# Convolutions ahead of the pooling branch, the samples' recurrence inside it, and one product of keys with q and k

## The chip, the core and the metric

The kernel runs on one core of a Trainium2 chip. Its time is the device time of one execution in microseconds; the figure that counts is the median of several runs. Five engines work side by side: TensorE (PE, with its weight loads as PEld), VectorE (DVE), ScalarE (ACT), GpSimd (POOL) and SyncE (SP), which here only issues DMAs. Each engine works through its own instructions in order and waits on semaphores for the others.

## What is computed

One inference step of a hybrid decoder layer, for a prompt of 1024 tokens and for 8 samples of 4 tokens each (1056 columns in all), everything in float32. Cut to what matters here:

```python
def mixer_layer(x, p_i, conv_hist, s0, pool_hist, pos0, ...):
    h = rmsnorm(x, norm_mix)
    q_r, k_r, v_r, z, a_r, b_r, u, gp, ga, gb = jnp.split(h @ w_in, IN_SPLITS, axis=-1)
    qkv, conv_new = causal_conv(concat([q_r, k_r, v_r]), conv_hist, conv_w)   # 4 taps, silu
    q, k = l2norm(q) * HEAD_K ** -0.5, l2norm(k)                              # 8 heads of 128
    g, beta = -exp(a_log) * softplus(a_r + dt_bias), sigmoid(b_r)
    o, s_new = gated_delta_chunked(q, k, v, g, beta, s0, chunk)               # needs k.k and q.k
    y_a = (rmsnorm(o, gdn_norm) * silu(z)) @ w_proj_a
    y_pool, pool_new = pool_mix(u, pool_hist, pos0, pool_w, pool_scale)       # windows 2, 4, 8, 16
    y_b = (y_pool * silu(gp)) @ w_proj_b
    m = sigmoid(ga) * y_a + sigmoid(gb) * y_b
    x = x + m @ w_out
    return x + sigmoid(rmsnorm(x, norm_ple) @ w_ple_gate) * (p_i @ w_ple_proj), ...
```

The prompt starts from empty state; each sample brings a convolution history, a pooling history and a 128x128 recurrent matrix for each head, and its new states are outputs too.

## The kernel before, in words

Activations lie with features on the 128 partitions and tokens along the row, in three chunks of 352 columns. A dense product takes one output tile of 128 features (`dense`, L378): each of the three chunks is 24 matmuls (`chunk`, L306), because each operand is split into a high and a low part in the format fp32r (`hh`, `hl` for activations, `wh`, `wl` for weights) and three of the four products are made for each of the eight 128-row blocks. So a dense tile is 72 matmuls of 352 columns. The weights of a tile come by a 512 KB DMA into one of two `wr` buffers (`fetch`), ScalarE copies them to `wh` and GpSimd subtracts to get `wl` (`split_w`), one tile ahead. Products inside the heads are plain float32 and appear in the trace as two passes of TensorE each; transposes are one pass.

The order of the instructions on every engine but SP is written out by hand through a planner (`Weave`, L74). It keeps a planned time for every engine from a table of costs (`COST`, and the ns handed to `mm`), runs the dense tiles as the main line, and between any two matmuls steps those side threads (Python generators) that are due by the planned time (`pump`). A `mark` is a planned finishing time, `until` and the lists that threads yield wait for marks. Rings hand out buffers (`take`, `give`). The planner's times only fix the order; on the chip each instruction waits for its real inputs.

The stages, in order:

1. Start (to about 59 us): `w_ple_proj` products, the first norm, splitting of h.
2. Convolutions and pooling (to about 546 us). For m = 0 to 7: the dense tile of u (`w_in` 32+m), whose evacuation by ScalarE fills the one buffer `up`; thread `windows` (DVE sums over 2, 4, 8 or 16 tokens, then `shi`, `slo`); at even m the group map of the previous group (`group_maps`, 36 matmuls); then the tiles k (8+m, through `conv_tile(m, 1)`), gate (40+m), q (m) and v (16+m). A conv tile is evacuated by ScalarE into `xr`; two DVE steps a chunk add the middle taps to `acc`, GpSimd adds `f`, ScalarE makes a tanh, DVE multiplies; the result goes to DRAM (`kq_d`, `v_d`). Buffers: two `xr`, three `f`, one `acc` for each chunk. Dense products have four PSUM banks here (`psd`).
3. Heads (to about 1143 us). The main line is 8 tiles of z, 15 of gates and 8 of `w_proj_b`, with two `psd` banks. Side threads take the heads in four pairs (`pair`, `decays`, `whole`, `queries`, `values`, `recurrence`): load k, transpose, products k.k, inverse of a triangular matrix (DVE), load q, products q.k, load v, a recurrence over 8 chunks of 128 tokens, output to `og_d`. All their big buffers are 19 slots of 4 KB a partition (`U_r`, `NSLOT`). Pair p+1 starts when pair p has all its slots (mark `have`). After them thread `samples` runs the recurrence of the 8 samples: it waits for the last pair's `have` and for z, takes seven slots and `en`, loads 4 MB of states in 256 KB pieces and writes them back, and ends in `osm` (mark `smp`).
4. At m = 2 to 7 of `w_proj_b` the program asks whether all heads and the samples are done; if so, or after the last tile, `heads_end` frees the heads' memory and the threads `reload` bring `og_d` back in 24 pieces (`rw`), split into `oh` and `ol`, the input of `w_proj_a`.
5. `w_proj_a`, `w_out`, the norm, `w_ple_gate`, final norm (to the end).

Of the kernel before, what the change touches and what calls it, by code (L numbers as in the profile page):

```python
# [18 lines left out]
P = 128  # L19
# [24 lines left out]
NSLOT = 19  # L44
# [190 lines left out]
def decoder_step(ctx, tc, A, O):  # L235
# [110 lines left out]
    order += [("pool_w", 3)] + [("w_in", 24 + m) for m in range(H)] + [("w_in", 49 + m) for m in range(2 * KT - 1)] + [("w_proj_b", m) for m in range(KT)]  # L346
# [340 lines left out]


    with pool("pw", 2) as pw, pool("cvt") as cv, pool("psab", 2, space=PSUM) as psab:
        wv.add(token_rates(ab, abf, psab))  # L690
        ring = lambda p, name, shape, n, dt=F32: Ring(wv, [p.tile(shape, dt, name=f"{name}{i}") for i in range(n)])
# [6 lines left out]
        yh_r, yl_r = (ring(cv, f"ys{x}", [P, CW], 3, F32R) for x in "hl")  # L698
# [57 lines left out]
        seg4 = lambda t: t.rearrange("p (s x) -> p s x", x=7)[:, :, 0:ST]  # L756

        def conv(n, c, o, h, j, xr, f):

            m = 8 * j + h  # L760
            c0, c1 = n * CW, (XW - 3 if n == 2 else (n + 1) * CW)
            if n < 2:
                S.copy(xr[:, 3 + c0:3 + c1], o)
            else:
                xs = xr[:, 3 + TP:XW]
                S.copy(xr[:, 3 + c0:3 + TP], o[:, 0:TP - c0])
                S.copy(xs.rearrange("p (s x) -> p s x", x=7)[:, :, 3:7],
                       o[:, TP - c0:CW].rearrange("p (s x) -> p s x", x=ST))
            yield "ps"
            act = yield from acc_r[n].take()  # L770
            yield
            acc = act[:, 0:c1 - c0]
            fc = f[:, c0:c1]
            S.activation(acc, xr[:, c0:c1], AF.Copy, scale=cw[:, m, 0:1])
# [7 lines left out]
            if n == 2:  # L782
                G.tensor_copy(cvp[:, m, :], xr[:, TP:TP + 3])
                SY.dma_start(O["conv_s"][:, m], xs)
# [281 lines left out]
    def recurrence(o):  # L1066
# [7 lines left out]
        for u in range(NU):  # L1074
# [27 lines left out]
            if u:  # L1102
                mm(po[:, P:2 * P], Fq[:, tok], st, 222)
# [657 lines left out]
```

## Time and profile before

| | us |
|---|---|
| median of 3 runs | 1467.9 |
| lowest and highest of them | 1463.51, 1471.36 |
| the profiled execution's own time | 1464.74 |
| its span, first to last instruction | 1463.0 |
| mean granted TensorE clock | 0.986 of 2.4 GHz |

The profile is one execution of the program. The page gives each engine's busy time; the views cut it by stretch of time, by line, by tile and by wait. In the name of a tile the buffer number is left out; helpers record all dense and head matmuls as L247, transposes as L251, all ScalarE, DVE and GpSimd work as L186 and DMA issues as L231, so groups are told apart by tile. Names of the heads' buffers appear as `U`. The end of a matmul is modelled: it includes the way through the array, so matmuls overlap in the listing, and the distance from one start to the next is what one costs. Most of the loss on TensorE is therefore read from counts of matmuls in a stretch, beside the idle time that the view shows.

### The profile page before, as it was taken

To read this page: it belongs to the slowest core of one execution; us is meant where nothing else is said; L and a number is where in the kernel's file an instruction comes from. 1 tells how busy PE (TensorE), PEld (TensorE's weight loads), DVE (VectorE), ACT (ScalarE), POOL (GpSimd) and SP (SyncE) were. 2 spreads that over 40 slices of the span, in tenths; PEclk is the share of its full clock that TensorE was granted. 3 is DMA by queue.
4 is the path that set the end of the run, shared out by engine and by line. 5 is a ranking of instruction groups with operands and counts; after the bars stand their busy time and mean duration, and the time that the engine had idled before them with its cause. 6 is when DMAs were issued, how large, how long until landed. Compare 5 with 4: busy or idle time off the path is not lost.

```text
span 1463.0 us, 24635 instructions
## 1 busy us (share of the span) xinstructions
PE 1410.1 (96%) x9266; PEld 1369.5 (94%) x9266; DVE 844.0 (58%) x1779; ACT 590.9 (40%) x1545; POOL 427.1 (29%) x353
## 2 busy tenths in 40 slices
PE   9899999999999998999999999999899699999996
PEld 8799999999999998999999999999799599999996
DVE  6675564565657653474663764665665554556655
ACT  6344444444444444536536436525101322324321
POOL 3524433334343441411313212301332011315100
PEclk9999999999999999999999999999999899999998
DMA  9223243142224228241441431495265644424132
GB/s 333 61 65 94 69 130 100 58 136 87 86 71 135 79 73 249 99 107 44 159 132 54 170 124 36 163 289 173 88 208 166 219 142 133 136 67 128 46 96 88
DMA packets 106235, 178.95 MB, mean 122 GB/s; under 512 B 19260, under 2 KB 78852, under 8 KB 106116
## 3 DMA queue, kind: packets, MB, share of 16 engines
q1 hardware_dynamic: 106116, 177.37, 37.9%
q8 instruction: 73, 1.20, 0.3%
q14 instruction: 46, 0.38, 0.1%
HBM read 119.92 MB, written 57.41 MB: 121 GB/s over the span
## 4 chain that ended last, share of the span: by engine, by line
PE 87%; DVE 7%; DMA 2%; ACT 2%; issue 1%; SPq 0%; POOL 0%; DVEq 0%; ACTq 0%; POOLq 0%
PE psd L247 73%; PE psr L247 6%; PE psg L247 5%; PE psg L251 2%; DVE U L186 1%; DMA rw<-og_d 1%; DVE win L186 1%; PE pse L247 1%; DVE hl L186 1%; DVE ol L186 0%; DMA xt<-in_xT_dram 0%; DVE x L186 0%; DVE sg L186 0%; DVE tm L186 0%; SPq L231 0%
## 5 line engine op out<-in xcount | busy, mean ns | idle before, releaser
L247 PE MATMUL psd<-hh,wh 128*128 128x352 f32 x1728 | 569.9, 330 | 2.6 <-DVE sg L186 2.0
L247 PE MATMUL psd<-hl,wh 128*128 128x352 f32 x1728 | 566.7, 328 | 0.0
L247 PE MATMUL psd<-hh,wl 128*128 128x352 f32 x1728 | 565.0, 327 | 0.0
L186 POOL TENSOR_TENSOR wl<-wr,wh 128x1024 fp32r<-128x1024 f32 (+1 forms) x87 | 207.3, 2383 | 551.8 <-ACT wh L186 508.5
L247 PEld LDWEIGHTS psd<-hh,wh 128*128 128x128 f32 x1728 | 326.8, 189 | 5.2 <-issue 2.1
L247 PEld LDWEIGHTS psd<-hl,wh 128*128 128x128 f32 x1728 | 327.3, 189 | 1.4 <-issue 0.2
L247 PEld LDWEIGHTS psd<-hh,wl 128*128 128x128 f32 x1728 | 326.7, 189 | 1.5 <-issue 0.5
L186 DVE SCALAR_TENSOR_TENSOR acc<-xr,cw,acc 128x352 f32<-128x352 f32 x144 | 123.6, 868 | 60.9 <-ACT acc L186 59.3
L186 POOL TENSOR_TENSOR acc<-acc,f 128x352 f32<-128x352 f32 (+1 forms) x72 | 78.6, 1092 | 118.9 <-DVE acc L186 84.3
L186 ACT CAST wh<-wr 128x1024 fp32r<-128x1024 f32 (+1 forms) x88 | 90.5, 1028 | 14.9 <-issue 7.4
L186 DVE SCALAR_TENSOR_TENSOR f<-f,acc 128x352 f32<-128x352 f32 (+1 forms) x72 | 60.9, 849 | 46.0 <-ACT f L186 46.0
L186 ACT ACTIVATE junk<-psg 128x128 f32<-128x128 f32 (+1 forms) x136 | 38.5, 283 | 85.8 <-PE psg L251 71.0
L247 PE MATMUL psd<-oh,wh 128*128 128x352 f32 x192 | 64.0, 333 | 7.6 <-ACT oh L186 7.6
L247 PE MATMUL psd<-ol,wh 128*128 128x352 f32 x192 | 64.5, 336 | 5.6 <-DVE ol L186 5.4
L186 ACT COPY xr<-psd 128x352 f32<-128x352 f32 (+1 forms) x96 | 34.0, 380 | 81.0 <-PE psd L247 80.9
L186 ACT ACTIVATE gt<-psd 128x352 f32<-128x352 f32 x69 | 32.5, 472 | 82.4 <-PE psd L247 69.8
L247 PE MATMUL psd<-oh,wl 128*128 128x352 f32 x192 | 63.6, 331 | 0.0
L186 ACT ACTIVATE f<-acc 128x352 f32<-128x352 f32 (+1 forms) x72 | 36.2, 503 | 47.1 <-POOL acc L186 32.4
L186 DVE SCALAR_TENSOR_TENSOR gt<-gt,psd 128x352 f32<-128x352 f32 x48 | 24.8, 516 | 49.1 <-ACT gt L186 33.6
L186 ACT COPY U<-psr 128x128 f32<-128x128 f32 (+1 forms) x68 | 18.1, 270 | 83.2 <-PE psr L247 35.0
L251 PE MATMUL psg<-cst,U 128*128 128x128 f32 (+3 forms) x272 | 40.7, 274 | 8.5 <-DVE U L186 5.2
L247 PE MATMUL psd<-gh,rh 128*128 128x352 f32 x144 | 46.8, 325 | 0.0
(256 smaller groups left out, 2564.0 us busy)
## 6 DMA issues: line engine op xcount, KB each, us to landing
wr<-in_w_in_dram SPq DMA_DIRECT2D x64, 512.0 KB, 3.9
kq_d<-f SPq DMA_DIRECT2D x16, 512.0 KB, 2.9
U<-kq_d SPq DMA_DIRECT2D x16, 512.0 KB, 5.5
xt<-in_xT_dram SPq DMA_DIRECT2D x6, 704.0 KB, 7.2
pp_d<-ppt SPq DMA_DIRECT2D x24, 176.0 KB, 5.8
yh_d<-ysh SPq DMA_DIRECT2D x24, 176.0 KB, 3.5
yl_d<-ysl SPq DMA_DIRECT2D x24, 176.0 KB, 2.6
tb_d<-gt SPq DMA_DIRECT2D x24, 176.0 KB, 1.8
```

The costliest lines, as they stand in the source:

```text
L186: return f(*a, **k)
L247: PE.matmul(o, l, r, start=start, stop=stop)
L251: PE.transpose(o, i, idn)
```

## The change

Three things are changed together.

- **Order.** All 24 conv tiles come first, head by head in the order q, k, v, with three `xr`, four `f` and two `acc` for each chunk; the planner drains its threads and the last convolution state is written. Then come the pooling tiles alone: u, at even m the group map, gate.
- **Samples.** `samples` keeps its instructions but runs as a side thread of the pooling stage, with buffers of its own in a pool `smp` and two PSUM rings of two banks (`sg`, `sr`), and waits neither for heads nor for z. Its last step no longer multiplies by silu(z): ScalarE writes `osm`, and after the last z tile GpSimd multiplies `osm` by `ssz`; the mark `smp` is set there.
- **Heads.** q and k of a head are loaded together into one buffer F of two rows (four such buffers of 8 KB; the 4 KB slots go from 19 to 13). The products k.k and q.k of a chunk become one matmul of 256 columns with k stationary, two of them to a PSUM bank; each bank is read by two DVE products of 256 columns. `queries` keeps only transposes and squares. v's slot and load come ahead of the inverse.

The diff, cut to its core (the body of `samples`, `group_maps` and `windows` is moved and is the same line for line where nothing is shown):

```diff
-NSLOT = 19
+NSLOT = 13
-    order = [("w_in", 48)]
+    order = [("w_in", 48)] + [("w_in", h + 8 * j) for h in range(H) for j in range(3)]
     for m in range(KT):
-        order += [("w_in", 32 + m)] + [("pool_w", m // 2 - 1)] * (m > 1 and m % 2 == 0)
-        order += [("w_in", 8 + m), ("w_in", 40 + m), ("w_in", m), ("w_in", 16 + m)]
+        order += [("w_in", 32 + m)] + [("pool_w", m // 2 - 1)] * (m > 1 and m % 2 == 0) + [("w_in", 40 + m)]
...
-        xr_r = ring(cv, "xr", [P, XW], 2)
-        f_r = ring(cv, "f", [P, XW], 3)
-        acc_r = [ring(cv, f"acc{n}_", [P, XW - 2 * CW], 1) for n in range(NCH)]
+        xr_r = pring(cv, "xr", [P, XW], 3)
+        f_r = pring(cv, "f", [P, XW], 4)
+        acc_r = [pring(cv, f"acc{n}_", [P, XW - 2 * CW], 2) for n in range(NCH)]
...
+        for h in range(H):
+            for j in range(3):
+                conv_tile(h, j)
+        wv.until()
+        SY.dma_start(O["conv_p"], cvp)
+    actx.close()
+    with pool("smp") as smp, pool("pw", 2) as pw, ExitStack() as pc:
+        g_r, r_r = banks(pc, "sg", 2), banks(pc, "sr", 2)
...
-        yield [("have", H // 2 - 1), ("z", H - 1)]
-        slots = []
-        for _ in range(7):
-            slots.append((yield from U_r.take()))
-        yield from en_r.take()
...
-        V.scalar_tensor_tensor(out=osm, in0=pf[:, 0:H * TS].rearrange("p (h t) -> p h t", t=TS), scalar=gn,
-                               in1=ssz.rearrange("p (h t) -> p h t", t=TS), op0=ALU.mult, op1=ALU.mult)
-        wv.mark("smp")
+            S.activation(osm, pf[:, 0:H * TS].rearrange("p (h t) -> p h t", t=TS), AF.Copy, scale=gn)
...
+        wv.add(samples())
         last, grp = None, None
         for m in range(KT):
...
-            conv_tile(m, 1)
-            conv_tile(m, 0)
-            conv_tile(m, 2)
...
     U_r = ring("U", [P, NU, P], NSLOT)
+    F_r = ring("F", [P, 2, TP], 4)
...
-            o.Fk = flat((yield from U_r.take()))
-            SY.dma_start(o.Fk, kq_d[o.h][1], ("k", o.h))
+            o.F = yield from F_r.take()
+            SY.dma_start(o.F[:, 1], kq_d[o.h][1], ("k", o.h))
+            SY.dma_start(o.F[:, 0], kq_d[o.h][0], ("q", o.h))
...
-            for g in range(2):
-                yield [("decay", o.h, g)]
+            for g in range(4):
+                yield [("decay", o.h, g // 2), ("q", o.h)]
                 pk = yield from g_r.take()
                 yield
-                for j in range(4):
-                    mm(pk[:, j * P:(j + 1) * P], o.Fk[:, tok], o.Fk[:, tok], 222)
-                V.tensor_tensor(out=o.nt[:, us], in0=units(pk), in1=en[:, i, us], op=ALU.mult)
+                for j in range(2):
+                    mm(pk[:, 2 * j * P:2 * (j + 1) * P], o.F[:, 1, tok], o.F[:, :, tok], 240)
+                V.tensor_tensor(out=o.nt[:, us], in0=pv[:, :, 1], in1=en[:, i, us], op=ALU.mult)
+                V.tensor_tensor(out=o.em[:, us], in0=pv[:, :, 0], in1=o.em[:, us], op=ALU.mult)
...
-                mm(pq[:, i * P:(i + 1) * P], o.Fk[:, tok], o.Fq[:, tok], 222)
-            V.tensor_tensor(out=em[:, us], in0=units(pq), in1=em[:, us], op=ALU.mult)
...
+                if h == H - 1:
+                    yield
+                    G.tensor_tensor(out=osm, in0=osm, in1=ssz.rearrange("p (h t) -> p h t", t=TS), op=ALU.mult)
+                    wv.mark("smp")
```

## Rows read from the trace of the kernel before

**Rows 1.** The page: busy us, share of the span and instructions of each engine.

```profile
PE 1410.1 (96%) x9266; PEld 1369.5 (94%) x9266; DVE 844.0 (58%) x1779; ACT 590.9 (40%) x1545; POOL 427.1 (29%) x353
```

**Rows 2.** Stretches: busy us (instructions) of PE, PEld, DVE, ACT, POOL; clock; DMA.

```profile
59.00:541.00 482.00, 480.68 (x3021) 479.18 (x3022) 283.77 (x402) 218.40 (x440) 183.62 (x173) 1.00 0.28 89
541.00:566.00 25.00, 19.80 (x111) 18.96 (x110) 11.88 (x21) 9.37 (x25) 7.14 (x5) 0.92 0.69 227
566.00:1025.00 459.00, 451.37 (x3324) 435.08 (x3323) 259.05 (x762) 220.65 (x807) 103.40 (x85) 1.00 0.42 133
1025.00:1143.50 118.50, 112.17 (x711) 103.28 (x709) 70.71 (x151) 15.01 (x33) 39.90 (x32) 0.99 0.47 153
1143.50:1171.50 28.00, 14.86 (x57) 12.79 (x56) 14.97 (x34) 12.50 (x33) 2.54 (x1) 0.72 0.77 252
```

**Rows 3.** Waits of PE, 1143.5 to 1171.5: total us, times, longest.

```profile
PE psd L247 <- ACT oh L186: 7.6, 1, 7.6
PE psd L247 <- DVE ol L186: 5.4, 3, 3.1
```

**Rows 4.** Groups of PE, 1025 to 1143.5.

```profile
L247 PE MATMUL psd<-hh,wl 128*128 128x352 f32 x161 | 53.6, 333 | 0.0
L247 PE MATMUL psr<-en,U 128*128 128x128 f32 x64 | 11.0, 298 | 1.5 <-DVE U L186 1.5
L247 PE MATMUL psg<-ue,kl 96*128 96x512 f32 x16 | 7.2, 452 | 0.6 <-DVE ue L186 0.6
```

**Rows 5.** Timeline of PE, heads stage: start us, us, what, count.

```profile
611.06 1.05 PE L247 MATMUL psg<-U,U 128*128 128x128 f32 x8
...
612.11 0.33 PE L247 MATMUL psd<-hl,wh 128*128 128x352 f32 x1
```

**Rows 6.** Tile psg on PE, 1000 to 1143: ns minimum/median/maximum, first and last start.

```profile
L247 PE MATMUL psg<-ue,kl x16: 393/474/501, 1065.8 to 1131.3; 96*128 96x512 f32 x16
L251 PE MATMUL psg<-cst,sq x12: 270/272/273, 1008.4 to 1017.1; 128*64 128x128 f32 x12
```

**Rows 7.** Timeline of SP's queue at 1040 us: the last output of a head.

```profile
1040.28 0.32 SPq L231 DMA_DIRECT2D og_d<-U  x1
```

**Rows 8.** Groups of PE, 1040.5 to 1143.5: count, busy us, mean ns, idle before.

```profile
L247 PE MATMUL psd<-hh,wl 128*128 128x352 f32 x144 | 48.0, 333 | 0.0
```

**Rows 9.** Groups of DVE, 60 to 541: the pooling windows.

```profile
L186 DVE TENSOR_TENSOR win<-up 128x1190 f32<-128x1190 f32 x8 | 11.2, 1398 | 44.5 <-ACT up L186 44.5
L186 DVE TENSOR_TENSOR slo<-y,shi 128x1056 fp32r<-128x1056 f32 x8 | 10.6, 1319 | 4.1 <-ACT shi L186 3.9
```

**Rows 10.** DMA issues, 1000 to 1143: count, KB each, median us to landing.

```profile
out_delta_s_dram<-U SPq DMA_DIRECT2D x8, 256.0 KB, 2.1
```

**Rows 11.** Stretches view: two conv tiles back to back.

```profile
104.00:127.00 23.00, 23.00 (x146) 23.00 (x146) 14.64 (x18) 13.22 (x27) 10.32 (x11) 1.00 0.25 74
```

**Rows 12.** Waits of PE, 541 to 566.

```profile
PE psg L251 <- DMA U<-kq_d: 3.3, 1, 3.3
PE psd L247 <- DVE sg L186: 1.9, 2, 1.0
```

**Rows 13.** Timeline of PE at the norm's broadcast product (352 columns, plain float32).

```profile
1292.31 0.76 PE L247 MATMUL pse<-dg,cst 88*128 88x352 f32 x2
...
1293.06 0.32 PE L247 MATMUL psd<-ml,wh 128*128 128x352 f32 x1
```

**Rows 14.** Groups of DVE, 566 to 1025: a product that reads a whole bank.

```profile
L186 DVE TENSOR_TENSOR U<-psg,en 128x512 f32<-128x512 f32 x16 | 11.0, 690 | 18.1 <-PE psg L247 16.7 <-DMA out_delta_p_dram<-st 1.1
```

**Rows 15.** Groups by line, 60 to 541: conv tiles' DVE and GpSimd work, weight split.

```profile
L186 DVE SCALAR_TENSOR_TENSOR acc<-xr,cw,acc 128x352 f32<-128x352 f32 x141 | 121.8, 874 | 60.9 <-ACT acc L186 59.3
L186 POOL TENSOR_TENSOR wl<-wr,wh 128x1024 fp32r<-128x1024 f32 (+1 forms) x43 | 101.3, 2357 | 175.5 <-ACT wh L186 151.7 <-ACT acc L186 9.5 <-issue 9.2
L186 POOL TENSOR_TENSOR acc<-acc,f 128x352 f32<-128x352 f32 (+1 forms) x70 | 76.7, 1096 | 114.3 <-DVE acc L186 82.2 <-ACT f L186 23.7 <-DVE y L186 3.1
L186 DVE SCALAR_TENSOR_TENSOR f<-f,acc 128x352 f32<-128x352 f32 (+1 forms) x69 | 59.4, 864 | 45.8 <-ACT f L186 45.8
```

More of the change, by code (lines that the diff above doesn't have):

```diff
@@ L754, in windows @@
             wv.mark("win", m)
[L756 to L770, printed above, removed]
[L771 to L778 removed]
+        R = 64
@@ new lines, in chain @@
+                pb = yield from g_r.take()
+                for a in range(2):
+                    mm(pb[0:96, a * P:(a + 1) * P], f3(x3[:, a]), r, 222)
+                if g:
+                    yield [("sn", g - 1)]
+                V.tensor_tensor(out=u3, in0=units(pb[0:96, 0:2 * P]),
+                                in1=d3[:, 0:8].rearrange("p (a g) -> p a g", a=2)[:, :, g].unsqueeze(2).broadcast_to([96, 2, P]),
+                                op=ALU.mult)
+                g_r.give(pb)
+                yield
@@ new lines, in chain @@
+                uu = r_
+                S.copy(ul, u3)
+                for a in range(2):
+                    V.tensor_copy(uu[32 * a:32 * a + 32], u3[32 * a:32 * a + 32, a])
+                yield
+                V.tensor_tensor(out=ul[32:64], in0=u3[32:64], in1=ul[32:64].bitcast(F32), op=ALU.subtract)
+                po = yield from g_r.take()
+                mm(po[0:R, 0:P], sk[:, g], uu, 222)
+                V.tensor_tensor(out=oo[:, g, :], in0=po[0:R, 0:P], in1=oo[:, g, :], op=ALU.add)
@@ new lines, in chain, with products @@
+                g_r.give(po)
+                wv.mark("ch", g)
+                yield [("kl",)]
+                yield from new_states(g)
+            def products(g):
+                pa = yield from r_r.take()
+                for i in range(16):
+                    if i % ZN == 0:
+                        yield
+                        c = slice(R * g + ST * i, R * g + ST * (i + ZN))
+                        V.tensor_copy(cols(0), s8(sq[:, 1, c]))
+                        V.tensor_tensor(out=cols(R), in0=s8(sq[:, 0, c]), in1=s8(gbs[:, g, ST * i:ST * (i + ZN)]), op=ALU.mult)
+                        yield
+                    if i % 4 == 0:
+                        yield [("sg", g, i // 4)]
+                    c = 60 + P * (i % ZN) - ST * i
+                    mm(pa[:, 0:P], zf[:, c:c + P], sgs[g % 2][i // 4][:, i % 4, :], 222, start=(i == 0), stop=(i == 15))
+                    if i % 2:
+                        yield AHEAD
+                wv.mark("pa", g)
+                return pa
@@ L785, in conv @@
+            wv.add(states(2))
+            wv.add(states(3))
+            for g in range(4):
+                pa = yield from products(g)
+                if g:
+                    yield [("ch", g - 1)]
+                wv.add(chain(g, pa))
+                yield
+            yield [("ch", 3), ("sn", 3)]
+            at[0] = 160
+            ss = t_([R, 4], "sss")[0:R]
+            for g in range(4):
+                S.activation(r_, oo[:, g, :], AF.Square, accum_out=ss[:, g:g + 1])
             yield
-            S.activation(fc, acc, AF.Tanh, scale=0.5)
+            ro = yield from out_scale(R, 4, ss, n2[:, 0, :], t_)
@@ L795, in conv @@
[L795 to L810 removed]
+            pf = yield from g_r.take()
```

558 lines of the change are left out of this document (254 added, 304 removed).

## The prediction

> **What bounds the kernel now.** I read the page first: TensorE is busy for 96% of the span, no other engine for more than 58% [rows 1]. So two questions decide: does the change take work from TensorE, and does it take away gaps? The stretches view shows where the gaps are. A dense pass (352 columns, fp32r) costs 480.68 us / 3021 = 0.159 us in the convolution and pooling stage, where TensorE hardly ever stands still; I use 0.160 [rows 2]. With that price a stretch's loss is its length less its passes. From 1143.5 to 1171.5 there are 57 passes, 9.1 us of work in 28.0 us: 18.9 us are lost, 13 as idle time and the rest because the clock was at 1.2 instead of 2.4 GHz for part of it, a mean of 0.72 [rows 2]. The waits name the cause: `oh` and `ol`, the reloaded outputs of the heads [rows 3]. From 1025 to 1143.5, the samples' stretch, I count three groups of about 161 dense passes (77.0 us), 128 passes of `psr` at 0.111, priced below (14.2), 16 of `ue` at an estimated 0.3 (4.8: between a dense pass scaled to 512 columns, 0.23, and the listed mean of 0.45) and 86 others of at most 0.111 (9.5): at most 105.5 us, so at least 13.0 us are lost, of which 118.5 - 112.2 = 6.3 show as idle [rows 2, 4]. From 541 to 566, where the heads begin, 111 passes are at most 17.8 us of 25: 7.2 lost [rows 2]. The 459 us of the heads show 7.6 us idle [rows 2]; the start and the end are not touched.
>
> **The reload, 17.9 us off.** Before, `heads_end` could not come before `smp`, and the samples' last product starts at 1131 [rows 6], when `w_proj_b` was nearly through; so all 24 pieces were reloaded with TensorE waiting. The heads themselves were done earlier: the last `og_d` leaves at 1040 [rows 7], and from there to 1143.5 three groups of 144 dense passes remain, exactly six tiles, 6 x 11.5 = 69 us [rows 8]. With `smp` set after the z tiles, the program can call `heads_end` near tile m = 2 or 3 of `w_proj_b`, and 28 us of reload fit beside 58 or more us of dense work. DVE, busy 71 of 118 us there with the samples, loses their part [rows 2]. I keep 1 us for the new PSUM banks. If heads ended 45 us later, that cover would be gone and all 18.9 us would be back. Bounds: 15 to 18.9. The same loads now queue on SP among the `tb` loads that evacuations need, so I charge 1 us (0 to 3).
>
> **The samples, 3.1 us off.** The same passes of TensorE, ScalarE, DVE and GpSimd work, 16 loads and 16 stores of 256 KB on SP move into the pooling stage. That stage has 16 dense tiles and 144 group-map passes, 16 x 11.5 + 23 = 207 us of TensorE without the samples; the chain's products ran from 1008 to 1131 us before, 123 us [rows 6], so it ends in time. What of the loss comes along? The 6.7 us that do not show as idle are short gaps between small products; they come along. Of the 6.3 us of idle I let half come along: these are steps whose DVE work was later than planned, and the pooling windows put 1.4 us instructions in their way [rows 9], but four PSUM banks, not two, serve the dense tiles. So 13.0 - 6.7 - 3.2 = 3.1 us. Bounds: from -8 (each of the 16 blocks of state products held up by half a window instruction, 0.7 us) to +13. SP is a queue in order: a state's reload waits for its store to land, 2.1 us [rows 10], four times in a row, and weights, `y_d` stores and pooling histories stand behind. Weights are fetched a tile ahead, 11.5 us; I cost this at nothing, and without that cover at 2 x 8 us.
>
> **Convolutions first, 1 us on.** No instruction is added; 24 tiles run back to back. The nearest row is a stretch with two back to back: TensorE is busy 23.00 of 23.00 us, DVE 14.64, GpSimd 10.32 [rows 11]. Nothing builds up over two tiles, and the rings get longer. I charge 1 us (0 to 6). The first conv tile follows the first gate tile a tile earlier than before; the weights are in the same two buffers, and I cost that at nothing. `conv_p` on SP now waits for the last tile's chain with pooling's loads behind it, while two weight tiles are already in: nothing.
>
> **Pooling alone.** Between the u tiles of two m stood four dense tiles, now one, sometimes with a group map. `windows` for a group of 16 is four sums of 1.4 us, then `y`, `shi` and `slo` of about 1.3 each: 9.5 us against 11.5 us of gate tile and four PSUM banks of 3.8 us [rows 2, 9]. Nothing, and up to 4 us with the samples on DVE.
>
> **Where the heads begin, 2 us off.** Of the 7.2 us, 3.3 are the wait for the first k, 1.9 group-map products waiting for DVE, and the rest the slower clock after them [rows 2, 12]. DVE then no longer has the last conv tiles; I take off 2 us. The wait for k stays: `v_d` and `conv_p` are gone from the queue ahead of it, and q loads stand only behind the first k. Bounds: 3 us worse to 7 us better.
>
> **The joint product, 0.6 us off.** Before, eight passes of 128 columns in plain float32 cost 1.05 - 0.16 = 0.89 us, 0.111 each, so k.k and q.k of a chunk cost 4 x 0.111 = 0.444 us [rows 5]. 256 columns are not in the trace. The nearest row on the other side is a 352 column product in plain float32: two passes and one dense pass take 1293.06 - 1292.31 = 0.75 us, so a pass is 0.295 [rows 13]. Float32 passes therefore grow with their columns, (0.295 - 0.111) / 224 = 0.82 ns each: 256 columns are 0.216, two passes 0.432. That saves 0.012 x 64 = 0.8 us at most; I take 0.6. The planner is told 240 ns for it, so its order runs some 12 us ahead of TensorE over the stage; DVE waits, which costs TensorE nothing as long as dense tiles follow. The Trainium skill (TensorE: Matmul & The Clock Gate, Back-to-back issue gap) lists 134 cycles for 128 columns and 262 for 256; by it two passes of 256 would be an estimated 0.218 us, and 64 products would save 14.5 us against the 0.444 of the trace. The page does not tell float32 apart; the 352 column row speaks against it here.
>
> **DVE and slots in the heads.** Four products of 512 columns (0.69 us [rows 14]) a head become eight of 256, at most 2.8 us more a head. DVE is busy 259 of 459 us there [rows 2], so TensorE pays nothing; the pairs' chain could grow by 22 us at most, against the 69 us above. Slots: after `whole` a pair held 12 of 19 and left 7, which the next pair needs for two k, two kt, two em and one nt; now it holds 8 of 13 and leaves 5, for two kt, two em and one nt, with k and q in F. The same point stops the next pair. The new wait for q precedes products only; behind it stands the pair's own chain. The final `osm` product of 256 columns is on GpSimd beside gate tiles: nothing.
>
> **Sum.** 17.9 - 1 + 3.1 - 1 + 2 + 0.6 = 21.6 us. The span goes from 1463.0 to 1441.4, the profiled time from 1464.74 to 1443.1. That execution was 3.2 us faster than the median of 1467.9, so the median goes to 1446.
>
> **Rivals.**
> - *The samples' losses vanish*: they meet a roomier stage, and the 9.9 us that I let come along do not. 1436.
> - *The samples disturb pooling*: 0.7 us at each of 16 blocks, 11 us; 1457. For it: DVE windows; against it: four banks.
> - *The reload stays*: the pairs need 45 us more, or the planner sees them done only at the last tile. 1446 + 17 = 1463. Against it: the count of slots.
> - *256 columns are cheap*: if float32 passes ran at the dense rate beyond 128 columns, a pass would be 0.160 x 256 / 352 = 0.116, a product 0.233, and 64 save 13.5 us: 1433. The 0.295 us row is against it. The table in the Trainium skill (TensorE: Matmul & The Clock Gate, Back-to-back issue gap) would have it so.
> - *The slower one, conv tiles no longer fit*: a conv tile needs on DVE 6 x 0.874 + 3 x 0.864 = 7.8 us and on GpSimd 2.36 + 3 x 1.10 = 5.7 us [rows 15]. If the two could not overlap at all it would take 13.5 us, 2.0 more than TensorE, 24 times: 48 us, 1494. It is slower than before from 0.9 us a tile. In the pair above they summed to 25.0 us in 23.0 and TensorE did not wait, so I hold it unlikely.
> - *The samples outlast pooling*, so that the change doesn't do what it says: at 2.2 times their 123 us the chain would take 270, 35 us beyond the 207 + 28 of pooling and samples together; 1481. Against it: the chain's idle steps were few.
>
> **How the numbers follow.** My forecast, 1446, has 0.50; samples vanish 0.18; samples disturb 0.14; reload stays 0.06; cheap columns 0.04; conv tiles 0.05; samples outlast 0.03. The range: the bounds summed in full on the good side (18.9 + 13 + 7 + 0.8) give 1428; on the bad side the reload at 15, its loads at 3, the samples at -8, the heads' begin at -3 and conv tiles at 6 would give 1472. They hardly fall together, so I end the range at 1462; above it lie the cases of conv tiles and of samples that outlast, half of the reload that stays, and such sums, some 0.15 in all. About 0.5%, 7 us, is what a measurement here can tell from no change, so faster means below 1460.6: 0.80, with nearly all of the first three and the cheap columns; same 0.12; slower 0.08.
>
> **What would show it.** After the change the stretch before `w_proj_a` should hold passes without waits for `oh` or `ol`, with `og_d` reloads beside `w_proj_b`; a 256 column product should be two passes 0.21 to 0.22 us apart; the conv stage should take 24 x 11.5 = 277 us; idle time in pooling should be some 3 us. I am wrong if `oh` waits remain, if conv tiles take over 12 us each, or if the joint products are near 0.12 us a pass.

## The result: no gain, 0.5% slower

The changed kernel takes 1475.8 us (median of 16 runs, 1469.66 to 1481.32) against 1468.0 us for the kernel before on the same chip (16 runs, 1463.51 to 1472.53). The ratio is 1.0051, with a 95% interval of 1.0034 to 1.0067. The forecast was 1446, with a range of 1428 to 1462. The profiled execution of the changed kernel took 1481.32 us, span 1479.5; that of before had a span of 1463.0. The profile of the changed kernel is thus of its longest execution, and of the 16.5 us between the spans 8 are in the medians; the runs below show the same stages with less noise.

The page of the changed kernel, busy us and share of the span, beside [rows 1]: TensorE has as much to do and is as busy.

```profile
PE 1418.8 (96%) x9138; PEld 1375.8 (93%) x9138; DVE 834.5 (56%) x1810; ACT 590.2 (40%) x1546; POOL 425.3 (29%) x354
```

So again the gaps decide. The loss of a stretch is counted as in the prediction, its length less its passes, with 0.160 us for a dense pass, 0.111 for a plain float32 pass of 128 columns, 0.2175 for one of 256 (below) and the other small products in proportion to their columns:

| stretch | loss before | loss after | difference |
|---|---|---|---|
| start, to 60 | 13.6 | 15.9 | +2.3 |
| convolutions and pooling, after with the samples (60 to 550; 60 to 613) | 2.6 | 37.1 | +34.5 |
| first 25 us of the heads | 7.7 | 7.7 | 0 |
| heads, to the last gate tile | 22.3 | 21.4 | -0.9 |
| from there to the first `w_proj_b` product (984 to 993; 1038 to 1069) | 3.5 | 14.0 | +10.5 |
| `w_proj_b`, before with the samples (to 1151; to 1181) | 25.0 | 8.8 | -16.2 |
| from `w_proj_a` on, before with the rest of the reload | 28.1 | 15.0 | -13.1 |

The differences add up to 17.1; the joint product takes 0.5 us off the passes. The start's 2.3 us need not come from the change: among the variants of the changed kernel below, which start alike, the same stretch differs by up to 2.4 us. The gain that was forecast for the reload is there, in the last two lines, together with the loss that the samples left behind. Two lines ate it: the samples lose more amid pooling than they ever lost behind the heads, and a stretch with no dense products opened ahead of `w_proj_b`.

The stretches view of the changed kernel (busy us and instructions of PE, PEld, DVE, ACT, POOL; granted clock; DMA):

```profile
59.00:340.00 281.00, 279.99 (x1765) 277.96 (x1763) 186.87 (x280) 161.13 (x338) 134.53 (x147) 1.00 0.30 93
340.00:510.00 170.00, 154.64 (x916) 144.90 (x915) 100.83 (x191) 42.92 (x105) 49.66 (x42) 0.92 0.33 104
...
460.00:480.00 20.00, 14.72 (x62) 13.35 (x61) 9.77 (x8) 2.13 (x4) 5.69 (x6) 0.74 0.14 53
...
1038.00:1069.00 31.00, 24.64 (x199) 21.39 (x198) 13.99 (x35) 9.79 (x34) 2.67 (x2) 0.89 0.49 171
1111.00:1120.00 9.00, 4.09 (x16) 3.80 (x15) 3.56 (x8) 3.36 (x7) 0.00 (x0) 0.71 0.95 321
```

The 24 convolution tiles run with no gap. The samples' stretch, 340 to 510, is 15.4 us idle, and its mean clock is 0.92 of 2.4 GHz: from 460 to 480, behind its longest wait, TensorE was granted 1.2 GHz for half of the time (0.74). By the mean, 0.08 of 170 us, an estimated 13.6 us, went to the slower clock, nearly as much as to idle time. What TensorE waits for there (total us, times, longest):

```profile
PE sg L247 <- DVE ue L186: 8.9, 4, 3.4
PE sg L251 <- ACT sjunk L186: 3.4, 1, 3.4
PE sr L247 <- DVE sv L186: 3.1, 5, 1.6
```

`ue` is one DVE instruction of 512 columns that usually takes 0.68 us. The timelines of GpSimd and of DVE (start, us) show what happened to it twice:

```profile
410.69 4.02 POOL L186 TENSOR_TENSOR sg<-sg,sa 128x512 f32<-128x512 f32 x4
411.48 3.79 DVE L186 TENSOR_TENSOR ue<-sa,ul 96x512 fp32r<-96x512 f32 x1
...
454.29 2.93 POOL L186 TENSOR_TENSOR wl<-wr,wh 128x1024 fp32r<-128x1024 f32 x1 [9.84 <-DMA yl_d<-ysl]
457.15 2.13 POOL L186 COPY sa<-sd 64x192 f32<-64x192 f32 x1
459.01 4.82 DVE L186 TENSOR_TENSOR ue<-sa,ul 96x512 fp32r<-96x512 f32 x1
459.25 4.03 POOL L186 TENSOR_TENSOR sg<-sg,sa 128x512 f32<-128x512 f32 x4
```

GpSimd scales the states of the next group, four tiles in a row (`sg<-sg,sa`), and `ue` ends only when the row ends. TensorE's waits behind these two are 2.4 and 3.4 us, 5.8 of the 8.9; the other two, 1.8 and 1.2 us, stand behind a `ue` of 2.85 and one of 2.44 us, each beside a single weight split (`wl`). In the kernel before all 16 scalings came one by one, most of them waiting for products of TensorE, and the longest `ue` took 1.56 us (the first two of GpSimd's timeline there):

```profile
1046.33 1.04 POOL L186 TENSOR_TENSOR en<-en,U 128x512 f32<-128x512 f32 x1 [3.27 <-PE psr L247]
1049.29 1.04 POOL L186 TENSOR_TENSOR en<-en,U 128x512 f32<-128x512 f32 x1 [1.92 <-PE psr L247]
```

Amid pooling GpSimd comes late from a weight split of 2.4 us or more in two of the four groups, the products are done by then, and the four run without a pause. Three kernels below (the hole, the reload's loads, the joint product undone) leave this stage as it is, or nearly so; they lose 32 to 33 us in it.

### The profile page after: what moved, and what is told of

Same layout as the page of the kernel before. It is cut to its first block, busy times and chain, and to the rows that moved or that the text cites. A ratio compares the mean times of both kernels' runs of the same rounds, so it can differ in the third digit from the quotient of the medians.

```text
span 1479.5 us, 24421 instructions
## 1 busy us (share of the span) xinstructions
PE 1418.8 (96%) x9138; PEld 1375.8 (93%) x9138; DVE 834.5 (56%) x1810; ACT 590.2 (40%) x1546; POOL 425.3 (29%) x354
## 4 chain that ended last, share of the span: by engine, by line
PE 84%; DVE 8%; DMA 3%; ACT 2%; issue 2%; SPq 1%; POOL 0%; DVEq 0%; ACTq 0%; POOLq 0%
PE psd L247 70%; PE psg L247 5%; PE psr L247 5%; PE psg L251 2%; DVE ue L186 1%; SPq L231 1%; DVE sg L186 1%; PE sr L247 1%; DVE big L186 1%; PE sg L247 1%; PE pse L247 1%; DVE hl L186 1%; DVE sv L186 1%; DMA pt<-in_pT_dram 1%; DMA xt<-in_xT_dram 1%
## 5 line engine op out<-in xcount | busy, mean ns | idle before, releaser
L247 PE MATMUL psd<-hh,wl 128*128 128x352 f32 x1728 | 571.1, 330 | 0.0
L247 PEld LDWEIGHTS psd<-hh,wh 128*128 128x128 f32 x1728 | 330.3, 191 | 10.3 <-DVE gt L186 5.2
L247 PEld LDWEIGHTS psd<-hh,wl 128*128 128x128 f32 x1728 | 330.4, 191 | 1.5 <-issue 0.2
L186 DVE SCALAR_TENSOR_TENSOR acc<-xr,cw,acc 128x352 f32<-128x352 f32 x144 | 106.5, 758 | 37.3 <-ACT acc L186 35.5
L186 POOL TENSOR_TENSOR acc<-acc,f 128x352 f32<-128x352 f32 (+1 forms) x72 | 73.6, 1028 | 121.1 <-DVE acc L186 92.2
L186 DVE SCALAR_TENSOR_TENSOR f<-f,acc 128x352 f32<-128x352 f32 (+1 forms) x72 | 70.8, 984 | 48.1 <-ACT f L186 48.1
L186 ACT ACTIVATE junk<-psg 128x128 f32<-128x128 f32 x128 | 36.3, 284 | 47.7 <-PE psg L251 46.0
L247 PE MATMUL psr<-uu,U 128*128 128x128 f32 x256 | 41.8, 285 | 5.1 <-ACT uu L186 2.0
L247 PE MATMUL psd<-gh,rl 128*128 128x352 f32 x144 | 46.5, 323 | 0.0
```

The costliest lines, as they stand in the source:

```text
L186: return f(*a, **k)
L247: PE.matmul(o, l, r, start=start, stop=stop)
```

## The experiments

Each time is a median; the kernel before, run beside each, had medians of 1466.4 to 1468.2. Ratios are to it.

**Convolutions first, alone.** The kernel before with only its loops and the order of its weights changed.

```diff
-    order = [("w_in", 48)]
+    order = [("w_in", 48)] + [("w_in", h + 8 * j) for h in range(H) for j in range(3)]
...
+        for h in range(H):
+            for j in range(3):
+                conv_tile(h, j)
         last, grp = None, None
         for m in range(KT):
...
-            conv_tile(m, 1)
...
-            conv_tile(m, 0)
-            conv_tile(m, 2)
```

> The kernel before with one of the three parts alone: the 24 convolution tiles run ahead of the pooling branch, with the rings and pools of before; samples, heads and products as before. If the part is free, as the prediction had it (1 us), it takes 1465 to 1471 us, as the kernel before, and the 24 tiles take 24 x 11.5 = 277 us without TensorE standing still. If the part is behind the slower result, it takes 1473 us or more, and the convolution stage shows waits of TensorE for psd, acc or f.

Measured: 1473.6 us, ratio 1.0048 (1.0030 to 1.0067). The time is that of the second case, the place is that of neither. Its stretches view:

```profile
59.00:340.00 281.00, 280.00 (x1764) 278.39 (x1763) 186.44 (x281) 161.50 (x340) 133.46 (x146) 1.00 0.29 92
984.00:1018.00 34.00, 26.42 (x130) 22.05 (x130) 13.16 (x42) 15.82 (x64) 2.35 (x1) 0.70 0.34 115
```

The convolution stage is free, even with the short rings of before. But 400 us later, between the gates and `w_proj_b`, 34 us without dense products have opened, where the kernel before has 9:

```profile
984.00:993.00 9.00, 7.07 (x55) 5.78 (x55) 5.03 (x12) 4.42 (x13) 2.36 (x1) 1.00 0.83 239
```

The 5.8 us are lost there: 20.0 against 3.5 by the count above, part of it given back because the reload then waits less. So a hole like that of the changed kernel (1038 to 1069) comes with this part of the change alone, through the order written out by the planner.

**The hole ahead of `w_proj_b`.** In the changed kernel the first two `w_proj_b` weights were asked for on SP ahead of the loads of y; the y loads follow, and after the hole comes the next weight (timelines of SP's queue and of PE, whose line is the first `w_proj_b` product):

```profile
1013.92 0.33 SPq L231 DMA_DIRECT2D wr<-in_w_proj_b_dram  x1
1017.63 1.05 SPq L231 DMA_DIRECT2D hh<-yh_d  x1
...
1068.59 0.33 SPq L231 DMA_DIRECT2D wr<-in_w_proj_b_dram  x1
...
1068.65 0.41 PE L247 MATMUL psd<-hh,wh 128*128 128x352 f32 x1
```

In the program's text, though, these weights are fetched in the last chunk of the gates, behind 32 of the 48 y loads of 180 KB. The planner's queue reckons with 220 bytes a ns (the kernel's own figure, `SY.rate`), some 26 us for the 32, holds the first product back by so much and fills the time with what the last pair of heads has. The edit asks for them in the first chunk:

```diff
                 f(w, n)
-                if n == NCH - 1:
-                    if raws:
-                        wv.run(split_w())
-                    fetch()
+                if n == 0:
+                    fetch()
+                elif n == NCH - 1:
+                    wv.run(split_w())
```

> The changed kernel with one thing changed: in the two stretches where two tiles are worked together, the next two weight tiles are asked for after the first chunk, ahead of the y loads, not after the last. Theory: the order written out by the kernel holds the first w_proj_b product back for a weight that it believes behind the y loads, so that for 30 us (1038 to 1068) TensorE has only the last heads' small products, and loses some 12 us there where the kernel before loses 5 in 9 us. Then this hole falls below 15 us and the time by 5 to 9 us, to 1467 to 1471. Rival: the last pair's chain is what takes the time and its products only run later without dense work beside them; then the hole moves toward the end of the heads, the reload comes later, and the time stays between 1473 and 1478.

Measured: 1466.9 us, 8.9 less than the changed kernel, ratio 0.9997 (0.9981 to 1.0012). The hole is gone: where 30.6 us lay between two dense products, 2.7 do (timeline of PE at the same place):

```profile
1031.51 0.32 PE L247 MATMUL psd<-hh,wl 128*128 128x352 f32 x1
...
1034.26 0.41 PE L247 MATMUL psd<-hh,wh 128*128 128x352 f32 x1
```

Heads and reload together lose 10 us less. The last `og_d` leaves at 1102, as before the edit (1103), in an execution whose heads began 7 us earlier: they end 6 us later by their own begin, a small part of the 30 us of the hole. The theory held. The same edit on the kernel before:

> The kernel before with weights asked for early, as in the run of that name on the changed kernel, and nothing else. The kernel before loses 3.5 us in its stretch without dense products ahead of w_proj_b (984 to 993). Theory: the 9 us that early weights brought the changed kernel lay in that stretch, which conv first had made long; then here it brings 0 to 4 us, 1464 to 1468. Rival: early weights are worth 9 us in any kernel, and are not part of what the change cost; then 1457 to 1461.

Measured: 1475.3 us, ratio 1.0053 (1.0036 to 1.0070): slower, which neither theory had. The hole is shorter here too (980 to 993.5 loses 2.1 us against 5.3), but the first evacuation of `w_proj_b` now meets the samples: its `tb` load stands on SP behind eight loads of states, and TensorE waits for it (SP's queue, then PE's waits, 990 to 1030):

```profile
988.81 1.82 SPq L231 DMA_DIRECT2D en<-in_sdelta_dram  x4
990.68 2.60 SPq L231 DMA_DIRECT2D U<-in_sdelta_dram  x4
993.66 0.33 SPq L231 DMA_DIRECT2D gt<-tb_d  x1
```

```profile
PE psd L247 <- DVE gt L186: 5.7, 1, 5.7
```

By the count, 993.5 to 1001 loses 6.5 us there and 0.4 in the kernel before. Besides, the last heads' output leaves at 1069.15, not at 1040.28 [rows 7], the samples' products start and end some 20 us later than in [rows 6], and after the last dense tile TensorE still waits for them and for the reload (PE's waits from 1143 to 1185):

```profile
PE psd L247 <- DVE ol L186: 4.0, 3, 2.7
PE psd L247 <- ACT oh L186: 3.9, 1, 3.9
```

This end, though, costs little more than it did: from the last dense product to 24 us into `w_proj_a` 21.7 us are lost against 19.9. So the same edit that fills the hole ran here into the samples' loads, which the change has moved away. Whether the heads' products in the hole are worth something as a head start isn't shown.

**The reload's loads.** In the changed kernel six `rw` loads stand on SP ahead of the `tb` load that an evacuation needs (first SP's queue, then the waits of PE and of DVE, 1107 to 1120):

```profile
1107.59 3.42 SPq L231 DMA_DIRECT2D rw<-og_d  x6
1111.05 1.85 SPq L231 DMA_DIRECT2D gt<-tb_d  x4
```

```profile
PE psd L247 <- DVE gt L186: 4.9, 1, 4.9
...
DVE gt L186 <- DMA gt<-tb_d: 11.4, 1, 11.4
```

```diff
+        yield [("tb", m)]
         rw = yield from rw_r.take()
...
         SY.dma_start(tb, tb_d[m][:, ns_(n)])
+        wv.mark("tb", m)
```

> The changed kernel with one thing changed: the reload of the heads' outputs issues its first loads only after the tb load that the first w_proj_b evacuation needs. Theory: the six rw loads ahead of it on SP cost TensorE the 4.9 us wait for gt and the slower clock behind it; then it falls by 3 to 6 us, to 1470 to 1473. Rival: the tb load waits anyhow, because its tile lies in the heads' memory, which comes free only when the last og_d has landed; then the wait for gt stays above 3 us and the time at 1474 to 1477.

Measured: 1472.2 us, 3.6 less than the changed kernel, ratio 1.0039 (1.0023 to 1.0055), an interval that overlaps the changed kernel's 1.0034 to 1.0067; clearer is that the wait for `gt` is 2.3 us in place of 4.9. The theory held for half of the wait; the rest fits the rival, since the load's buffer lies in the heads' memory, but this wasn't tested further.

**The samples: GpSimd's row and DVE.** First the scaling moved off GpSimd:

```diff
-                    G.tensor_tensor(out=sgs[g % 2][i], in0=sgs[g % 2][i], in1=gls[...]..., op=ALU.mult)
+                    for s in range(4):
+                        sv = sgs[g % 2][i][:, s]
+                        S.activation(sv, sv, AF.Copy, scale=gls[:, g, 4 * i + s:4 * i + s + 1])
```

> The changed kernel with one thing changed: the scaling of the samples' states (16 tiles of 128x512, four in a row on GpSimd for each of four groups) goes to ScalarE, 64 instructions of 128 columns. Theory: the four GpSimd instructions in a row hold up the DVE instruction that makes ue (3.8 and 4.8 us where 0.7 is usual), and TensorE waits 8.9 us for ue and then runs at the slower clock. Then ue takes 0.7 to 1.0 us everywhere, the waits for ue fall below 2 us, and the time falls by 9 to 16 us, to 1460 to 1467. Rival: the samples lose their time amid pooling because their products are small and each depends on the one before; then ue waits move to other steps of the chain and the time stays between 1472 and 1476.

Measured: 1456.1 us, 19.7 less than the changed kernel, ratio 0.9921 (0.9904 to 0.9938): faster than the kernel before. First the stretch, then PE's waits, 340 to 510:

```profile
340.00:510.00 170.00, 163.87 (x1046) 156.88 (x1045) 102.37 (x211) 67.34 (x180) 35.27 (x28) 0.99 0.40 126
```

```profile
PE sg L251 <- ACT sjunk L186: 3.6, 1, 3.6
PE sg L247 <- DVE ue L186: 1.4, 1, 1.4
```

More than expected; the mean clock of the stretch, 0.92 in the changed kernel, is 0.99. But the edit took away GpSimd's results as well as its work. So the work alone was put back, from constants into a tile that nobody reads:

```diff
+                S.copy(scr[0:R, 0:P], pa[R:2 * R, 0:P])
...
+                    G.tensor_tensor(out=units(scr), in0=units(cst[:, 0:512]), in1=gn..., op=ALU.mult)
```

> As the run with the scaling on ScalarE, and beside it the same four GpSimd instructions of 128x512 in a row, at the same point of each group's chain, from constants into a tile that nobody reads: no step of the samples depends on them. Theory (GpSimd keeps DVE out of memory while it runs): ue takes 2 to 5 us again in some groups, TensorE waits 5 us or more for ue, and the time comes back to 1465 to 1476. Rival (the chain waited for GpSimd's results and its queue, not for memory): ue stays at 0.7 us and the time within 3 us of 1456.

Measured: 1462.3 us, 6.2 more than without the idle instructions, ratio 0.9962 (0.9949 to 0.9975), between the two cases. No `ue` was held by a row, and one ran inside a row for its usual 0.68 us, which the theory had not allowed (timelines of GpSimd and of DVE):

```profile
410.31 4.88 POOL L186 TENSOR_TENSOR scr<-cst,gn 128x512 f32<-128x512 f32 x4 [7.28 <-ACT scr L186]
412.49 0.68 DVE L186 TENSOR_TENSOR ue<-sa,ul 96x512 fp32r<-96x512 f32 x1
```

The longest new wait of TensorE, 2.2 us, is for a weight split in GpSimd's queue (`wl`).

Three more edits of the changed kernel, one step each: `ue` on ScalarE; the small copy `x3`, which stands behind the weight split and ahead of the row, on ScalarE; each scaling issued just ahead of its own `ue`.

```diff
-                    V.tensor_tensor(out=ue, in0=d3[...]..., in1=ul[...]..., op=ALU.mult)
+                    for s in range(4):
+                        c = 8 + 4 * (i % 2) + s
+                        S.activation(ue[:, s], ul[:, i // 2].bitcast(F32), AF.Copy, scale=d3[:, c:c + 1])
```

> The changed kernel with ue made on ScalarE, four instructions of 128 columns where DVE made one of 512; the states' scaling stays on GpSimd, four in a row. The run with idle GpSimd instructions gave back only 6 of the 20 us, and its instructions did not meet ue, so what held the chain is open. Theory (DVE's ue, which reads two operands from SBUF, is held up while GpSimd works): the waits for ue, 8.9 us, vanish and the time falls to 1456 to 1466. Rival (GpSimd's queue: the copy x3 and the scalings stand behind a weight split, and the chain waits for them): the waits turn up at another step of the chain and the time stays at 1471 to 1477.

```diff
-                G.tensor_copy(x3, X[:, g]...)
+                S.copy(x3, X[:, g]...)
```

> The changed kernel with the copy x3, which stands behind the weight split in GpSimd's queue and ahead of the next product of the chain, on ScalarE; the scalings stay on GpSimd, behind the split and so four in a row. Theory (DVE held up by GpSimd's memory work): ue still takes 3 us or more beside a row of scalings, and the time stays at 1470 to 1477. Rival (GpSimd's queue): the time falls to 1456 to 1466.

```diff
 # new_states, ahead of ue; the loop of four in chain() is gone
+                    G.tensor_tensor(out=sgs[g % 2][i], in0=sgs[g % 2][i], in1=gls[...]..., op=ALU.mult)
                     ue_ = yield from ue_r.take()
```

> The changed kernel with each scaling still on GpSimd, but issued just ahead of the ue of the same tile, so that no four stand in a row. Theory (DVE is held up for as long as GpSimd has work in a row): no ue takes more than 3 us, the waits for ue fall to 2 to 5 us and the time to 1460 to 1470. Rival (GpSimd's queue and results): each addition to a state now waits for a scaling, 1.04 us, and 16 of them cost up to 16 us: 1474 to 1490.

Measured: 1464.4 (ratio 0.9983, 0.9970 to 0.9996), 1456.1 (0.9927, 0.9911 to 0.9942) and 1458.7 us (0.9948, 0.9930 to 0.9966). With `ue` on ScalarE its waits are gone, as the theory had it, but now a copy of 16 columns is caught beside three scalings, and TensorE waits 4.3 us for such copies, 2.8 of them at once (first the timelines of GpSimd and DVE, then PE's waits):

```profile
406.89 3.03 POOL L186 TENSOR_TENSOR sg<-sg,sa 128x512 f32<-128x512 f32 x3
407.01 2.94 DVE L186 COPY sv<-sq 128x16 f32<-128x16 f32 x1
```

```profile
PE sr L247 <- DVE sv L186: 4.3, 3, 2.8
```

The run with `x3` on ScalarE came out at the rival's time, against the theory's number. It still has two rows of four, but here GpSimd is the one that gives way: they take 6.28 and 6.47 us, and the longest `ue` 1.83 (first GpSimd's timeline, then tile `ue` on DVE, ns minimum, median, maximum):

```profile
403.21 6.28 POOL L186 TENSOR_TENSOR sg<-sg,sa 128x512 f32<-128x512 f32 x4
```

```profile
L186 DVE TENSOR_TENSOR ue<-sa,ul x16: 673/681/1834, 398.3 to 480.4; 96x512 fp32r<-96x512 f32 x16
```

So the queue is not what TensorE waits for in the changed kernel: no wait of this stage names GpSimd, and `x3` ended at 459.3 while `r` on DVE, the other input of the next product, ended at 464.5. Nor does a row as such cost the time: I took it to be a `ue` that is caught for a whole row. That left the question whether any other order would do as well, hence two controls that shift this stage without touching the row, `ue` or `x3`: a step on ScalarE moved behind the squares, and the samples started a tile later.

```diff
-            yield [("gbs",)]
-            S.activation(gls, gbs[...]..., AF.Exp)
-            yield
-            V.tensor_tensor(out=gbs[:, 4:8], in0=gbs[:, 4:8], in1=gbs[:, 0:4], op=ALU.subtract)
             for j in range(3):
...
+            # the same lines here, behind the loop
             vs, dl, nd = yield from token_scalars(...)
```

> The changed kernel with only that step of the decay row moved; the states' scaling stays on GpSimd, four in a row behind a weight split, and ue on DVE. A control for the four runs that each moved one of these and brought 11 to 20 us: this shifts the order of the same stage without touching them. Theory (the loss is the place where GpSimd's row meets ue): if ue is still caught by a row for over 3 us, TensorE's waits for ue stay near 9 us and the time is 1468 to 1474, the 4 us of the row's load less. Rival (the changed kernel's order in this stage was unlucky in some other way, and any other order is 15 us better): 1453 to 1460 although ue is still caught.

```diff
-        wv.add(samples())
...
             dense("w_in", 32 + m, hhi, hlo, ev_u)
+            if m == 0:
+                wv.add(samples())
```

> The changed kernel with the samples started one dense tile later in the pooling stage, nothing else: a second control, in which every step of the samples meets other steps of pooling. Theory: the time goes with the longest ue: with one or more over 3 us 1466 to 1478, with none over 3 us 1455 to 1462. Rival: no such link, a time of 1453 to 1462 with ue caught for over 3 us, or of over 1468 without.

Measured: 1472.8 (ratio 1.0033, 1.0020 to 1.0046) and 1463.7 us (0.9971, 0.9954 to 0.9989). In the first control no `ue` was itself caught for over 3 us, but TensorE still waited 8.0 us for it, 6.2 of them at once, since an instruction of 32 columns ahead of it on DVE was caught (first the timelines of DVE and GpSimd, then PE's waits):

```profile
454.86 4.32 DVE L186 SCALAR_TENSOR_TENSOR y<-win,up 128x32 f32<-128x32 f32 x1
455.10 4.02 POOL L186 TENSOR_TENSOR sg<-sg,sa 128x512 f32<-128x512 f32 x4
459.36 0.68 DVE L186 TENSOR_TENSOR ue<-sa,ul 96x512 fp32r<-96x512 f32 x1
```

```profile
PE sg L247 <- DVE ue L186: 8.0, 3, 6.2
```

In the second no `ue` was caught at all, and the time was just above the range that theory gave for that. A copy of 16 columns (3.97 us) and an addition of 3 were caught instead, and TensorE waited for the steps behind them (the same views for the addition):

```profile
472.93 4.24 DVE L186 TENSOR_TENSOR y<-y,up 128x3 f32<-128x3 f32 x1
473.12 4.03 POOL L186 TENSOR_TENSOR sg<-sg,sa 128x512 f32<-128x512 f32 x4
```

```profile
PE sg L247 <- DVE sa L186: 4.5, 2, 2.6
```

So my link with the longest `ue` was too narrow: a product, a copy, an addition and a step of 32 columns were caught, all of them copies or with two operands in SBUF. A step that reads one of its operands from a PSUM bank (`sg<-sg,psd`) ran for its usual 0.51 us inside the changed kernel's first row, at 411.05. The losses from 60 us to the end of pooling, by the count above: 37.1 in the changed kernel, 31.1 and 25.8 in the controls, 20.3 with `ue` on ScalarE, 20.4 with idle rows, 16.9 with `x3` on ScalarE, 15.6 spread, 15.3 with the scaling on ScalarE. Shown is that the meeting costs TensorE time where it happens. How much of the 20 us belongs to it is not: the second control has four rows in place of two, TensorE waits 2.3 and 2.6 us behind what they caught, nearly as in the changed kernel, and still it is 12 us faster. The wait for the squares, 3.4 us (`sjunk`), is missing there; the rest isn't accounted for. So a mere shift of this stage can be worth up to some 12 us, and the gains of 11 to 20 us of the four edits may hold a part of that.

**The joint product, undone.**

```diff
-                    mm(pk[:, 2 * j * P:2 * (j + 1) * P], o.F[:, 1, tok], o.F[:, :, tok], 240)
+                    for a in range(2):
+                        c = (2 * j + a) * P
+                        mm(pk[:, c:c + P], o.F[:, 1, tok], o.F[:, a, tok], 222)
```

> The changed kernel with the joint product undone: each 256 column product of a key tile is two products of 128 columns, with k and q side by side as before. A joint product takes two passes of 0.2175 us in the changed kernel's trace, a pair of single ones 4 x 0.111 = 0.444 us. Theory: undoing it costs 64 x 0.009 = 0.6 us, so 1473 to 1479 us, not to be told from the changed kernel but for what the different order of the heads does. Rival (256 columns are cheap where others run beside them): 1485 us or more.

Measured: 1479.7 us, ratio 1.0082 (1.0068 to 1.0097); 3.9 more than the changed kernel, beyond the 0.6 of the products, so some 3 us are of something else, by elimination another order of the heads; far from the rival's 1485. The changed kernel's timeline gives the pass directly, 4 passes and one dense pass from 655.16 to 656.19, (1.03 - 0.16) / 4 = 0.2175 us:

```profile
655.16 1.03 PE L247 MATMUL psg<-F 128*128 128x256 f32 x4
655.84 0.51 PE L247 MATMUL psd<-hh,wl 128*128 128x352 f32 x1
656.19 0.32 PE L247 MATMUL psd<-hh,wh 128*128 128x352 f32 x1
```

**Together.** Scaling on ScalarE, `tb` first and weights early in one kernel:

> The changed kernel with all three: the states' scaling on ScalarE, the first tb load ahead of the reload, weights early. Alone they brought 19.7, 3.6 and 8.9 us against the changed kernel's 1475.8. If they are separate causes they add up to 32 us: 1441 to 1447. If they overlap (scaling on ScalarE alone already left no wait at the reload's start: the 6.8 us lost there had gone), 1446 to 1453.

Measured: 1448.6 us, ratio 0.9867 (0.9851 to 0.9884), 27.2 less than the changed kernel. They overlap by 5 us, the second case's number but not its reason: with the scaling alone TensorE still waits 5.3 us for `gt` at the reload's start. By the count, from the first product of the heads to `w_proj_a` the changed kernel loses 48.7 us, 44.0 with `tb` first, 38.4 with early weights and 38.4 with all three, so these two overlap. On top of this, the decay row used later (the edit of the first control):

> The version with the three fixes, and the samples' decay row used one step later: ScalarE squares q and k first and takes the row's exponential behind that, so that it no longer waits 6.9 us for the row's load with the squares and a weight cast queued behind. Theory: TensorE's wait of 4.2 us for the squares goes, and 1 to 3 us of slower clock behind it: 1441 to 1446. Rival: the squares themselves, eight of 0.27 us with a readout each, are what TensorE waits for, or the step that needs the row waits instead: 1447 to 1451.

Measured: 1448.3 us, ratio 0.9867 (0.9840 to 0.9893): nothing, the rival's number but not its reason. TensorE still waits for the squares, and with the row out of the way ScalarE waits for the store of the last convolution tile (waits of PE and ACT at the samples' start):

```profile
PE sg L251 <- ACT sjunk L186: 4.8, 1, 4.8
...
ACT sjunk L186 <- DMA v_d<-f: 3.6, 1, 3.6
```

By the order of the pools in the program the tile that ScalarE writes lies where the convolution's buffers were. Last, the three fixes with the samples started one tile later:

> The three fixes, and the samples started one dense tile later. Moving the decay row did not shorten TensorE's wait for the squares (4.8 us): with the row out of the way ScalarE waited 3.6 us for the last convolution tile's v_d store, whose source lies where the samples' tiles are put. Theory: a tile later (11.5 us) that store has landed, the wait for the squares is gone, and the time falls by 4 to 6 us, to 1443 to 1446. Rival: the samples then end later and meet other pooling steps, which costs as much; 1447 to 1453.

Measured: 1444.6 us, ratio 0.9847 (0.9833 to 0.9860), the best of all kernels here: 21.8 us below the kernel before and 31.3 below the changed one. The wait for the squares is gone. PE's waits from 340 to 520:

```profile
PE sr L247 <- DVE sv L186: 1.4, 1, 1.4
PE sg L247 <- DVE ue L186: 1.2, 2, 1.0
```

## Why the prediction was wrong, step by step

- **The reload**: the mechanism was right, `heads_end` came at tile m = 2, and no wait for `oh` or `ol` is left. The term that was mis-sized is "its loads", charged at 1 us (0 to 3): the stretch from 1111 to 1120 loses 6.8, 4.9 of it the wait for `gt`. The saving was 19 - 6.8, some 12 us, not 16.9.
- **The samples**: this is the step that failed. "The same passes of TensorE, ScalarE, DVE and GpSimd work" moved, at 9.9 us of loss; they lost 34.5, and some 30 in the three kernels that leave the stage alone. I priced the windows' DVE time at 0.7 us a block and put GpSimd at nothing without a reason, though [rows 15] show weight splits of 2.36 us on its queue all through this stage. What the runs show in its place: where a split comes in between, GpSimd's four scalings lose the pauses between them, a DVE step is caught for the whole row (3.8 and 4.8 us), and TensorE waits and then runs at the slower clock. With the scaling on ScalarE the stage loses 15.3 us, 12.7 more than before, not far from the 9.9. How much of the gap is these rows and how much the order in other ways stays open, as the second control shows. The rival "samples disturb pooling" had the place, but another mechanism and less than half of the price, 11 us.
- **Convolutions first, 1 us**: right for its own stage (279.99 of 281.00 us busy, DVE and GpSimd some 3% of the time busier than in [rows 11]). Wrong for the kernel: the part alone costs 5.8 us, in the order between the gates and `w_proj_b`. The prediction had no step for what a shift of planned times does to an order 400 us on; it took the heads' stage as given.
- **Heads' begin, 2 us off**: nothing came; the wait for k is 4.8 us in place of 3.3 [rows 12].
- **The joint product, 0.6 us**: right, 0.2175 us a pass against 0.216 forecast. The row of 352 columns [rows 13] decided rightly against the table of the Trainium skill (TensorE: Matmul & The Clock Gate, Back-to-back issue gap), by which the prediction had worked out 14.5 us.
- **DVE and slots**: right; the heads up to the last gate tile lose 21.4 against 22.3.

By these terms: 21.6 forecast, less 5 (reload's loads), 25 (samples), 10 (the hole) and 2 (heads' begin) is -20, near the -16.5 between the two spans; the terms are single executions and estimates, good to a few us. That four small edits bring 1444.6 doesn't make the forecast of 1446 right: it was for a kernel without them.

## What to carry to other kernels

Work that is moved into another stage must be priced on every engine that it shares there, not on the bottleneck alone: here a row of GpSimd instructions could hold up a DVE step for as long as the row lasted, and whoever stood behind that step. Where an order is written out from planned times, look at the seams between stages after every change ahead of them, for a stretch in which the main line's products are missing. The same edit can help one kernel and harm another: ask which loads it will meet in the queue. And one control that only shifts a stage tells how much of a gain may be the shift itself.

## What the hardware showed that I had not expected

DVE instructions could be held for a whole row of GpSimd instructions, not for one of them: `ue` 3.79 and 4.82 us where 0.68 is usual, an instruction of 32 columns 4.32, an addition of 3 columns 4.24, each beside four scalings of together 4.0 us. The Trainium skill (SBUF — State Buffer, SBUF: two separate sides) says that a DVE instruction with two inputs in SBUF and a GpSimd instruction that reads SBUF exclude one another for the whole of the instruction that came first. The traces agree that one waits for the other. By the sentence a DVE instruction would wait for one scaling of 1.0 us; here the waiting instruction did not get its turn between the four. In two kernels it did: with `x3` on ScalarE the rows took 6.28 and 6.47 us and DVE's instructions ran between their parts, and among the idle rows of 4.4 to 4.9 us a `ue` took its usual 0.68. What decides between the two wasn't found.
